# RWKV-7 recurrence on one core: each head's state placed by the head's parity instead of the chunk's, even and odd heads multiplied in turn, and values centred before the recurrence

## The chip, the core and the metric

The kernel runs on one NeuronCore of one Trainium2 chip. Its engines are TensorE (PE), VectorE (DVE), ScalarE (ACT), GpSimd (POOL) and SyncE (SP), which only issues transfers. The metric is device time in microseconds; lower is better. Instructions of one engine are executed in the order in which the program's scheduler has put them, so an instruction that waits holds up all that stand behind it on that engine.

## The reference

Two layers, each a token mixer and a dense SwiGLU, for 256 frames of width 2048 in fp32. The change lies in the first mixer, RWKV-7 with 32 heads of 64. A head keeps a 64x64 state S; every frame does

```
S_t = S_{t-1} diag(w_t) + (S_{t-1} a_t) b_t^T + v_t k_t^T      y_t = S_t r_t
mu  = mean(y);  var = mean((y - mu)^2)                          # over a head's 64 values
y   = (y - mu) * rsqrt(var + 64e-5) * lnx_g + lnx_b
y   = y + sum(r * k * r_k) * v                                  # the bonus, with the plain v
out = (y * g) @ w_o
```

S is linear in v, and so is y. If every v of a head has its mean over the head's 64 values taken off beforehand, y comes out with mean zero.

## The kernel before, in words

All weight products are GEMMs in split precision (`Stream.gemm`, lines 158 to 187): each block of 128x512 weights is cast to a rounded half (ACT, L149), the remainder is taken (DVE, L150), and three matmuls of 512 columns (L182 to L184) are made for each of two groups of 128 frames. Side work is written as generators that take a step after every three GEMM matmuls (`tick`), and the scheduler then fixes one order of instructions for each engine. Weights come in by transfers that SP issues (L194), half a megabyte each.

The recurrence is done in chunks of 64 frames by matrix products. The work is cut into 8 units, unit i being a group of 8 heads (512 columns) and a half of the frames (128 frames, that is two chunks c = 0 and 1). Four generators work on it, one unit behind the other:

- `prepare` (L565 to L673) makes the decays, the scaled keys and receptances, transposes them on PE (L635, L649), copies the transposes out of PSUM on ACT (L643 in eight copies, L654 in four) and multiplies them into one 128x128 block per head and chunk (L665, masked by DVE at L668 into `M`).
- `solve` and `merge` (L679 to L781) invert a triangular matrix per head and chunk with 32x32 products (L742, L749, L759, L775).
- `chain` (L792 to L848) carries the state. For each chunk: the block of M times the stacked tile `sv` (values on one half of the partitions, state on the other; L820), plus state times receptance (L823), a copy (ACT, L826), the inverse (L829), a copy (L831), the new state (L834, then DVE L841 or L843 and L844) and the output (L836, copied by L845).
- `post` (L850 to L901) norms each head's output (L858 to L888), transposes it (L896, L900), and `halve` splits it for the output GEMMs.

In `chain` the partition half depends on the chunk: `vs, us = half[c], half[1 - c]`. In chunk 0 all eight heads have their values on partitions 0 to 63 and their state on 64 to 127, in chunk 1 the other way round. So all eight products of L823, and all eight of L829, use the same half of the rows of the PE array and write the same half of the partitions:

```
for h, hs in enumerate(hsl):
    mm(pb[vs, hs], far[us, h, 0:C], sv[us, hs], start=h == 0, stop=False)      # L823
...
for h, hs in enumerate(hsl):
    mm(pu[us, hs], TT[us, h, :], vu[us, hs], start=True, stop=True)            # L829
```

`values` (L783) has SP load the values of a chunk twice (`sv`, `vu`), 64 rows of 512 each, from the DRAM copy `vdram`, which the GEMMs of v wrote (L529).

## Time and profile before

| | |
|---|---|
| runs | 2623.15, 2627.87, 2628.25 us; median 2627.87 us |
| profiled execution | 2622.87 us |
| its span, first to last instruction | 2621.1 us |
| PE busy | 2574.1 us (98%) |
| DVE busy, ACT busy | 1675.0 us (64%), 1481.8 us (57%) |
| the recurrence beside the first GEMMs of its output | from about 250 to 620 us of the span |

The profiled execution is shorter than the median by 5.0 us. Busy time of PE overlaps within itself: matmuls are pipelined, so the mean length of one matmul is longer than the distance from one to the next. How long a group of matmuls takes is therefore best read from the chain of work that ended last, which follows PE from start to start. An fp32 product is recorded as two matmuls, so eight products are x16.

### The profile page before, as it was taken

The numbers are of one execution on the slowest core, as the hardware profiler recorded it, in microseconds if no ns is written. First come the engines' busy times: TensorE is split into PE (matmuls) and PEld (weight loads), VectorE is DVE, ScalarE is ACT, GpSimd is POOL, SyncE is SP. The second block draws the span as 40 slices with busy tenths as digits, with TensorE's granted clock in tenths as the row PEclk, the third lists the DMA queues.
The fourth block names the chain that finished last, engine by engine and source line by source line (L and its number), as shares of the span: only waits on it lengthen the run. The fifth ranks groups of instructions, "written<-read, shape, count | busy, mean of one in ns | idle before, by whom it ended". The sixth has DMA issues, their size and how long they took to land.

```text
span 2621.1 us, 40943 instructions
## 1 busy us (share of the span) xinstructions
PE 2574.1 (98%) x15160; PEld 2110.4 (81%) x15160; DVE 1675.0 (64%) x2965; ACT 1481.8 (57%) x2869; POOL 92.2 (4%) x69
## 2 busy tenths in 40 slices
PE   7999999999999999999999999999999999999998
PEld 5788777778888888888888888888888888888887
DVE  7885888877555555555556677676755555555554
ACT  6665787876545454544455656555554545454444
POOL 0000010100000000000001010010000000000000
PEclk9999999999999999999999999999999999999999
DMA  6676323335666666655556666664666666665554
GB/s 193 181 212 215 111 86 102 105 114 154 192 186 192 187 192 186 192 193 192 189 190 205 201 201 185 184 203 155 188 189 189 190 188 192 187 192 190 195 193 161
DMA packets 253945, 468.46 MB, mean 179 GB/s; under 512 B 22248, under 2 KB 32696, under 8 KB 253744
## 3 DMA queue, kind: packets, MB, share of 16 engines
q1 hardware_dynamic: 250448, 463.10, 58.2%
q10 hardware_dynamic: 3136, 2.74, 0.3%
q8 instruction: 119, 1.95, 0.3%
q14 instruction: 82, 0.67, 0.1%
q0 software_dynamic: 160, 0.00, 0.0%
HBM read 457.37 MB, written 4.23 MB: 176 GB/s over the span
## 4 chain that ended last, share of the span: by engine, by line
PE 92%; ACT 4%; DVE 2%; issue 1%; DMA 1%; POOL 0%; SPq 0%; POOLq 0%; ACTq 0%; DVEq 0%
PE mm L182 28%; PE mm L184 28%; PE mm L183 28%; PE bg L997 1%; ACT xb L643 1%; PE bg L829 1%; DVE wl L150 1%; PE bg L820 1%; PE bg L665 1%; PE bg L836 1%; ACT Bs L867 1%; PE bg L312 1%; PE bg L834 1%; PE bg L823 0%; DVE xmf L376 0%
## 5 line engine op out<-in xcount | busy, mean ns | idle before, releaser
L150 DVE TENSOR_TENSOR wl<-st,wh 128x512 fp32r<-128x512 f32 (+1 forms) x1648 | 1129.8, 690 | 813.1 <-ACT wh L149 806.1
L149 ACT CAST wh<-st 128x512 fp32r<-128x512 f32 (+1 forms) x1648 | 1015.8, 622 | 952.2 <-DVE wl L150 697.3
L182 PE MATMUL mm<-wh,xb 128*128 128x512 f32 x2048 | 804.6, 393 | 0.0
L184 PE MATMUL mm<-wh,xb 128*128 128x512 f32 x2048 | 800.9, 391 | 0.0
L183 PE MATMUL mm<-wl,xb 128*128 128x512 f32 x2048 | 800.5, 391 | 0.0
L182 PEld LDWEIGHTS mm<-wh,xb 128*128 128x128 f32 x2048 | 385.0, 188 | 79.5 <-issue 3.3
L184 PEld LDWEIGHTS mm<-wh,xb 128*128 128x128 f32 x2048 | 384.8, 188 | 78.8
L183 PEld LDWEIGHTS mm<-wl,xb 128*128 128x128 f32 x2048 | 385.0, 188 | 75.9
L183 PE MATMUL mm<-wl,xa 128*128 128x512 f32 x768 | 305.3, 398 | 3.0 <-DVE wl L150 1.5
L182 PE MATMUL mm<-wh,xa 128*128 128x512 f32 x768 | 306.7, 400 | 0.0
L184 PE MATMUL mm<-wh,xa 128*128 128x512 f32 x768 | 305.0, 397 | 0.0
L184 PE MATMUL mm<-wh,hb 128*128 128x512 f32 x448 | 174.5, 390 | 0.0
L183 PE MATMUL mm<-wl,hb 128*128 128x512 f32 x448 | 174.5, 390 | 0.0
L182 PE MATMUL mm<-wh,hb 128*128 128x512 f32 x448 | 174.5, 390 | 0.0
L183 PEld LDWEIGHTS mm<-wl,xa 128*128 128x128 f32 x768 | 145.2, 189 | 33.0 <-DVE wl L150 3.2
L184 PEld LDWEIGHTS mm<-wh,xa 128*128 128x128 f32 x768 | 145.0, 189 | 30.0 <-issue 0.2
L182 PEld LDWEIGHTS mm<-wh,xa 128*128 128x128 f32 x768 | 145.4, 189 | 28.8 <-issue 1.0
L182 PEld LDWEIGHTS mm<-wh,hb 128*128 128x128 f32 x448 | 84.1, 188 | 17.5
L183 PEld LDWEIGHTS mm<-wl,hb 128*128 128x128 f32 x448 | 84.1, 188 | 17.5
L184 PEld LDWEIGHTS mm<-wh,hb 128*128 128x128 f32 x448 | 84.1, 188 | 17.3
L1181 POOL TENSOR_TENSOR n<-n,pw 128x8 f32<-128x8 f32 x24 | 47.2, 1968 | 409.0 <-DVE n L1180 409.0
L1224 ACT ACTIVATE sc<-sc,nm 128x128 f32<-128x128 f32 x64 | 28.7, 449 | 26.6 <-DVE nm L1223 26.6
(293 smaller groups left out, 1941.7 us busy)
## 6 DMA issues: line engine op xcount, KB each, us to landing
st<-in_f_w_gu_dram SPq DMA_DIRECT2D x352, 512.0 KB
st<-in_f_w_d_dram SPq DMA_DIRECT2D x176, 512.0 KB
st<-in_b_w_in_dram SPq DMA_DIRECT2D x128, 512.0 KB
st<-in_a_w_rkv_dram SPq DMA_DIRECT2D x96, 512.0 KB
st<-in_a_w_o_dram SPq DMA_DIRECT2D x32, 512.0 KB
st<-in_b_w_o_dram SPq DMA_DIRECT2D x32, 512.0 KB
cb<-cdram SPq DMA_DIRECT2D x4, 1024.0 KB
x<-in_x_dram SPq DMA_DIRECT2D x12, 256.0 KB
```

Of the source, the lines that this page charges most:

```text
L149: nc.scalar.copy(hi[:rows, :n], st)
L150: nc.vector.tensor_tensor(lo[:rows, :n], st, hi[:rows, :n].bitcast(F32), op=ALU.subtract)
L182: nc.tensor.matmul(ps[t][:, :n], xh[:rows, c], wh, start=b == 0, stop=False)
L183: nc.tensor.matmul(ps[t][:, :n], xh[:rows, c], wl, start=False, stop=False)
L184: nc.tensor.matmul(ps[t][:, :n], xl[:rows, c], wh, start=False, stop=b == kts - 1)
L312: nc.tensor.transpose(tp[:, i * T + t * P : i * T + (t + 1) * P], src[:, t, c : c + P], ident)
L643: nc.scalar.copy(dst, tpv[half[q], :, c, :])
L665: mm(pm[c][:, h * P : (h + 1) * P], fkb[us, b * 4 + h, :], far[us, b * 4 + h, :], start=True, stop=True)
L820: mm(pb[us, hs], M[:, c * 8 + h, C : 2 * C], sv[:, hs], start=True, stop=True)
L829: mm(pu[us, hs], TT[us, h, :], vu[us, hs], start=True, stop=True)
L1181: nc.gpsimd.tensor_tensor(n8[:, :], n8[:, :], pw[:, :], op=ALU.pow)
L1224: nc.scalar.activation(sc[:, c], sc[:, c], AF.Exp, bias=nm[:, t : t + 1], accum_out=nm[:, 2 + t : 3 + t])
```

## The change

A unit's head h = 2p + q has its state on partition half q, in both chunks, and its values on the other half. With that:

- the transposes come out of PE with even heads on one half of the partitions and odd heads on the other, which is where they are wanted, so that they are copied in 2 and 2 instructions instead of 8 and 4 (L661, L669 of the changed kernel), and the chunk's decay in 1 instead of 4 (L607);
- the products of L840 and L846 (before: L823, L829) are written in turn, an even head, an odd head, and so on (`turns`); the other products of the chain run over the four even heads and then over the four odd ones;
- what was one instruction on 64 rows of 512 becomes two on 64 rows of 4x64 for even and odd heads (kb, the state's update, the copies of the output, the loads of values), one copy becomes 128 rows of 256 (L844), and one is divided between ACT (L848) and DVE (L849);
- the values are centred once after the GEMM of v (`centred`), kept in a second DRAM array `wdram`, and the recurrence uses these. The norm then needs no mean: one square over 128x512, one reduction and one multiplication by the scale take the place of eight squares with a bias and eight scalings with a bias on ACT. The plain values are loaded again for the bonus (`vn`).

The diff, cut to its core:

```
+            def centred(vt, at):
+                v8 = vt[:, :].rearrange("p (h n) -> p h n", n=N)
+                m8 = lw.tile([P, 8], F32, name="m8")
+                nc.vector.tensor_reduce(m8[:, :], v8, AX.X, ALU.add)
+                nc.vector.tensor_scalar(m8[:, :], m8[:, :], -1.0 / N, None, op0=ALU.mult)
+                yield
+                wt = pre.tile([P, 2, T], F32, name="f2")[:, :, :].rearrange("p i n -> p (i n)")
+                nc.vector.tensor_tensor(
+                    wt.rearrange("p (h n) -> p h n", n=N), v8, m8[:, :].unsqueeze(2).broadcast_to([P, 8, N]), op=ALU.add
+                )
+                nc.sync.dma_start(wdram[at], wt)
...
-                    for c in range(2):
-                        for q in range(2):
-                            nc.scalar.activation(wc[half[c], q:8:2], pc[half[q], c:8:2], AF.Exp)
+                    nc.scalar.activation(wc[:, :], pc[:, 0:8], AF.Exp)
...
-                        nc.vector.scalar_tensor_tensor(
-                            kb[half[1 - c], c, :], kk[half[c], :], 0.5, Wi[half[c], :], op0=ALU.mult, op1=ALU.mult
-                        )
+                        for q in range(2):
+                            nc.vector.scalar_tensor_tensor(
+                                par(kb[half[q], c, :], q), par(kk[half[c], :], q), 0.5, par(Wi[half[c], :], q), op0=ALU.mult, op1=ALU.mult
+                            )
...
-                        for c in range(2):
-                            for q in range(2):
-                                dst = far[half[1 - c]].rearrange("f (p j) n -> f p j n", j=2)[:, :, q, j * C : (j + 1) * C]
-                                nc.scalar.copy(dst, tpv[half[q], :, c, :])
+                        dst = far.rearrange("f (c p) n -> f p c n", c=2)[:, :, :, j * C : (j + 1) * C]
+                        nc.scalar.copy(dst, tp[:, :].rearrange("f (p c t) -> f p c t", p=4, c=2))
...
-                        for q in range(2):
-                            dst = fkb[half[1 - c]].rearrange("f (p j) n -> f p j n", j=2)[:, :, q, :]
-                            nc.scalar.copy(dst, tkv[half[q], :, :])
+                        nc.scalar.copy(fkb[:, 4 * c : 4 * c + 4, :], tk[:, :].rearrange("f (p t) -> f p t", p=4))
...
-                a, b = u2.tile([P, 512], F32, name="sv"), u4.tile([P, 512], F32, name="vu")
+                a, b = u2.tile([P, 512], F32, name="sv"), u2.tile([P, 512], F32, name="vu")
                 r0 = t * P + c * C
                 for d in (a, b):
-                    nc.sync.dma_start(d[half[c], :], vdram[r0 : r0 + C, g * 512 : g * 512 + 512])
+                    for q in range(2):
+                        nc.sync.dma_start(par(d[half[1 - q], :], q), par(wdram[r0 : r0 + C, g * 512 : g * 512 + 512], q))
...
+                        heads = [(q, p, 4 * c + p, hsl[2 * p + q], slice(p * N, p * N + N)) for q in range(2) for p in range(4)]
+                        turns = [heads[4 * (j % 2) + j // 2] for j in range(8)]
-                        for h, hs in enumerate(hsl):
-                            mm(pb[us, hs], M[:, c * 8 + h, C : 2 * C], sv[:, hs], start=True, stop=True)
+                        for q, p, s_, hs, ps_ in heads:
+                            mm(pu[half[q], ps_], M[:, q * 8 + s_, C : 2 * C], sv[:, hs], start=True, stop=True)
                         if not first:
-                            for h, hs in enumerate(hsl):
-                                mm(pb[vs, hs], far[us, h, 0:C], sv[us, hs], start=h == 0, stop=False)
+                            for q, p, s_, hs, ps_ in turns:
+                                mm(pb[half[1 - q], ps_], far[half[q], s_, 0:C], sv[half[q], hs], start=p == 0, stop=False)
-                        nc.scalar.copy(vu[us, :], pb[us, :])
-                        for h, hs in enumerate(hsl):
-                            mm(pu[us, hs], TT[us, h, :], vu[us, hs], start=True, stop=True)
+                        u = u1.tile([P, 256], F32, name="u")
+                        nc.scalar.copy(u[:, :], pu[:, 0:256])
+                        for q, p, s_, hs, ps_ in turns:
+                            mm(pu[half[q], 256 + p * N : 256 + p * N + N], TT[half[q], s_, :], u[half[q], ps_], start=True, stop=True)
                         yield
-                        nc.scalar.copy(vu[us, :], pu[us, :])
+                        nc.scalar.copy(par(vu[half[0], :], 0), packed(pu[half[0], 256:512]))
+                        nc.vector.tensor_copy(par(vu[half[1], :], 1), packed(pu[half[1], 256:512]))
...
-                            mm(pb[vs, hs], M[:, c * 8 + h, 0:C], vu[:, hs], start=first, stop=first or h == 7)
+                            mm(pb[half[1 - q], ps_], M[:, q * 8 + s_, 0:C], vu[:, hs], start=first, stop=first or p == 3)
...
-                                nc.vector.tensor_tensor(new, pu[vs, :], sv[us, :], op=ALU.add)
-                                nc.vector.tensor_tensor(h4(new), h4(new), w, op=ALU.mult)
-                        nc.scalar.copy(Y[vs, :], pb[vs, :])
+                        for q in range(2):
...
+                                    nc.vector.tensor_tensor(new, old, par(sv[half[q], :], q), op=ALU.add)
+                                nc.vector.tensor_tensor(new, old, w, op=ALU.mult)
+                        for q in range(2):
+                            nc.scalar.copy(par(Y[half[c], :], q), packed(pb[half[1 - q], 0:256]))
...
+                vn = u1.tile([P, 512], F32, name="vn")
+                nc.sync.dma_start(vn[:, :], vdram[t * P : (t + 1) * P, g * 512 : (g + 1) * 512])
-                for h, hs in enumerate(hsl):
-                    nc.scalar.activation(y2[:, hs], Y[:, hs], AF.Square, bias=m8[:, h : h + 1], accum_out=r8[:, h : h + 1])
+                nc.scalar.activation(y2[:, :], Y[:, :], AF.Square)
+                nc.vector.tensor_reduce(r8[:, :], h4(y2[:, :]), AX.X, ALU.add)
-                for h, hs in enumerate(hsl):
-                    nc.scalar.activation(Y[:, hs], Y[:, hs], AF.Identity, scale=r8[:, h : h + 1], bias=m8[:, h : h + 1])
+                nc.vector.tensor_tensor(h4(Y[:, :]), h4(Y[:, :]), b8(r8[:, :]), op=ALU.mult)
```

The scheduler's order shows at three places what this moves. The first is PE in one chunk of the chain that is not a unit group's first. Before (L820, L823, L829, L834 and L836 as above; rows of GEMM matmuls between them):

```order
L820 MATMUL bg<-sv,xb_2535 64x64 x8
L823 MATMUL bg<-sv,xb_2535 64x64 x8
L184 MATMUL mm<-wh,xa_1478 128x512
L182 MATMUL mm<-wh,xa_1477 128x512
L183 MATMUL mm<-wl,xa_1477 128x512
L184 MATMUL mm<-wh,xa_1478 128x512
L829 MATMUL bg<-vu,TT_2551 64x64 x8
```

And in the changed kernel (L836 answers to L820 before, L840 to L823, L846 to L829, L852 to L834, L854 to L836):

```order
L836 MATMUL bg<-sv,xb_2580 64x64 x8
L840 MATMUL bg<-sv,xb_2580 64x64 x8
L846 MATMUL bg<-u,TT_2599 64x64 x8
L182 MATMUL mm<-wh,xa_1478 128x512
L183 MATMUL mm<-wl,xa_1478 128x512
L184 MATMUL mm<-wh,xa_1479 128x512
L854 MATMUL bg<-vu,xb_2580 64x64 x4
L182 MATMUL mm<-wh,xa_1478 128x512
L183 MATMUL mm<-wl,xa_1478 128x512
L852 MATMUL bg<-vu,xb_2580 64x64 x8
L854 MATMUL bg<-vu,xb_2580 64x64 x4
```

The inverse (L846) stands right behind the state product (L840) here, with no GEMM matmul between, since it now waits for L836 alone, and four output products of the even heads stand ahead of the state products L852.

The second is ACT from the norm of one unit to the preparation of the next. Before (L867 the squares, L643 and L654 the copies of the transposes, L882 the scaling):

```order
L867 ACTIVATE Bs,r_3893<-Y,m_3748 128x64 x7
L743 COPY Xs<-bg 128x256
L867 ACTIVATE Bs,r_3893<-Y,m_3748 128x64
L643 COPY xb_2534<-bg 64x4x64 x8
L654 COPY WW<-bg 64x4x128 x4
L149 CAST wh<-st 128x512
```

And in the changed kernel (L661 and L669 the copies of the transposes):

```order
L149 CAST wh<-st 128x512
L757 COPY Xs<-bg 128x256
L661 COPY xb_2580<-bg 128x4x2x64 x2
L669 COPY WW<-bg 128x512
L149 CAST wh<-st 128x512
L669 COPY WW<-bg 128x512
```

Twelve copies on half of the partitions have become four on all of them, and the eight squares are gone from ahead of them.

The third is DVE around the copy that the change gives to it (L849), in the changed kernel, with what each row waits for:

```order
L634 SCALAR_TENSOR_TENSOR WW<-kk,WW 128x512 [waits Activation_49]
L719 TENSOR_TENSOR E<-E 128x2x2 [waits DVE_49]
L150 TENSOR_TENSOR wl<-st,wh 128x512 [waits DMAHW6_49,Activation_49]
L723 TENSOR_REDUCE E<-E 128x2 [waits DVE_49]
L849 COPY vu<-bg 64x4x64 [waits Activation_49]
L719 TENSOR_TENSOR E<-E 128x3x3 [waits DVE_49]
```

The copy waits for ACT (for L848, the other half of the same copy), and stands in DVE's queue behind a remainder of weights (L150); before there was no instruction of DVE between L829 and L834.

## Rows read from the trace of the kernel before

**Rows 1.** The page: busy time of each engine over the span, and the engines' shares of the chain of work that ended last.

```profile
PE 2574.1 (98%) x15160; PEld 2110.4 (81%) x15160; DVE 1675.0 (64%) x2965; ACT 1481.8 (57%) x2869; POOL 92.2 (4%) x69
...
PE 92%; ACT 4%; DVE 2%; issue 1%; DMA 1%; POOL 0%; SPq 0%; POOLq 0%; ACTq 0%; DVEq 0%
```

**Rows 2.** Busy time in stretches of the span. Columns: start and end, length, then busy us (instructions) of PE, of its weight loads, of DVE, ACT and POOL, then PE's granted clock as a share of full speed, the share of the transfer engines, GB/s. The first row is the end of the GEMMs of v, the others the recurrence.

```profile
160.00:250.00 90.00, 89.77 (x417) 74.48 (x416) 53.28 (x90) 47.22 (x86) 3.17 (x5) 1.00 0.79 234
250.00:300.00 50.00, 47.54 (x296) 37.99 (x294) 42.42 (x83) 35.58 (x74) 2.31 (x2) 1.00 0.51 151
300.00:350.00 50.00, 47.43 (x863) 36.94 (x858) 40.55 (x86) 36.08 (x92) 4.90 (x4) 0.97 0.27 83
350.00:400.00 50.00, 47.13 (x661) 36.57 (x660) 40.66 (x94) 41.47 (x105) 6.31 (x5) 0.97 0.28 89
400.00:450.00 50.00, 49.14 (x718) 39.45 (x716) 39.45 (x85) 37.89 (x94) 5.59 (x5) 1.00 0.35 101
450.00:500.00 50.00, 47.81 (x923) 37.95 (x921) 42.79 (x97) 43.56 (x123) 5.20 (x4) 1.00 0.33 104
500.00:550.00 50.00, 48.57 (x691) 38.09 (x691) 42.27 (x89) 40.75 (x103) 6.16 (x5) 1.00 0.34 104
550.00:600.00 50.00, 48.26 (x696) 38.25 (x695) 30.61 (x69) 31.61 (x76) 1.94 (x1) 1.00 0.36 110
600.00:650.00 50.00, 48.99 (x233) 39.79 (x232) 42.50 (x79) 37.33 (x94) 3.24 (x2) 1.00 0.57 170
```

**Rows 3.** The chain of work that ended last, through one chunk: start us, us, what.

```profile
325.86 1.07 PE bg L820 x16
326.93 1.07 PE bg L823 x16
328.00 0.43 PE mm L183
328.43 0.24 PE mm L184
...
329.13 1.07 PE bg L829 x16
```

**Rows 4.** Groups of PE instructions by line: output<-inputs, rows*columns of the array, output shape, count | busy us, mean ns of one | idle us of PE just before them, and who ended it.

```profile
L823 PE MATMUL bg<-sv,xb 64*64 64x64 f32 x192 | 13.7, 222 | 0.0
L829 PE MATMUL bg<-vu,TT 64*64 64x64 f32 x256 | 18.3, 222 | 0.4 <-ACT vu L826 0.4
```

**Rows 5.** The same chain as in rows 3, other products on PE. L573: 128 columns of weights, 2 columns streamed. L635: transposes of 128x128. L742: 32x32, four heads' quarters of the array in turn. L759: 32x32, two quarters in turn. L665: 64 rows by 128 columns, the two halves of the rows in turn.

```profile
271.25 0.88 PE bg L635 x8
...
303.52 1.05 PE bg L742 x64
...
312.96 0.62 PE bg L759 x32
313.58 1.10 PE bg L665 x16
...
388.64 1.05 PE bg L573 x8
```

**Rows 6.** Groups by line as in rows 4: ACT's copies, squares and scalings of the recurrence, and the PE groups that waited for them.

```profile
L665 PE MATMUL bg<-xb,WW 64*128 64x128 f32 x256 | 28.4, 291 | 2.8 <-ACT WW L654 2.3
...
L643 ACT COPY xb<-bg 64x256 f32<-64x256 f32 x64 | 23.4, 366 | 3.1 <-PE bg L635 2.3
...
L882 ACT ACTIVATE Y<-Y,m,r 128x64 f32<-128x64 f32 x64 | 22.4, 428 | 1.7 <-DVE m L880 1.6
...
L654 ACT COPY WW<-bg 64x512 f32<-64x512 f32 x32 | 18.5, 580 | 0.8
...
L649 PE MATMUL bg<-cst,xb 128*128 128x128 f32 x64 | 10.1, 280 | 3.2 <-ACT xb L643 2.7 <-DVE xb L638 0.5
...
L831 ACT COPY vu<-bg 64x512 f32<-64x512 f32 x16 | 9.3, 581 | 13.6 <-PE bg L829 13.5
...
L743 ACT COPY Xs<-bg 128x256 f32<-128x256 f32 x16 | 5.9, 367 | 6.6 <-PE bg L742 6.5
...
L896 PE MATMUL bg<-cst,Y 128*128 128x128 f32 x32 | 5.5, 285 | 1.0 <-DVE Y L888 1.0
...
L577 ACT ACTIVATE rr<-kk 128x512 f32<-128x512 f32 x8 | 5.0, 628 | 1.8 <-DVE kk L575 1.8
...
L900 ACT COPY x<-bg 128x512 f32<-128x512 f32 x8 | 4.7, 584 | 0.6 <-PE bg L896 0.5
```

**Rows 7.** Groups by line as in rows 4: DVE on 64 rows of 512, on 128 rows of 256, and a reduction.

```profile
L628 DVE SCALAR_TENSOR_TENSOR xb<-kk,Wi 64x512 f32<-64x512 f32 x16 | 11.0, 686 | 0.5
...
L734 DVE TENSOR_TENSOR El<-Dg,cst 128x256 f32<-128x256 f32 x16 | 6.7, 420 | 1.5 <-PE bg L742 1.4
...
L858 DVE TENSOR_REDUCE m<-Y 128x8 f32<-128x512 f32 x8 | 5.4, 680 | 6.9 <-ACT Y L845 6.8
```

**Rows 8.** The same chain as in rows 3, at the end of the recurrence: the eight squares of the last unit.

```profile
599.83 1.05 ACT Bs L867 x6
...
601.08 1.52 ACT Bs L867 x9
```

**Rows 9.** Transfers. From the page: ACT's queue, the one with the smallest pieces (packets, MB, share of 16 engines' span). From the issues of line 789: duration ns min/median/max of issuing one, first and last start.

```profile
q10 hardware_dynamic: 3136, 2.74, 0.3%
...
L789 SPq DMA_DIRECT2D vu<-vdram x16: 445/451/588, 167.6 to 541.3; - x16
```

More of the change, by code (lines that the diff above doesn't have):

```diff
@@ L339, in hybrid_kernel @@
         vdram = dram.tile([T, D], F32, name="vdram")
+        wdram = dram.tile([T, D], F32, name="wdram")
         loraw = {}
@@ L528, in hybrid_kernel @@
                     nc.scalar.copy(vt[:, :], ps[t][:, :])
-                    nc.sync.dma_start(vdram[t * P : (t + 1) * P, g * 512 : (g + 1) * 512], vt[:, :])
+                    at = slice(t * P, (t + 1) * P), slice(g * 512, (g + 1) * 512)
+                    nc.sync.dma_start(vdram[at], vt[:, :])
+                    S.add(centred(vt, at))
             S.until(lambda: not S.act and not S.pend)
@@ L673, in prepare @@
                     done.add(("prep", i))
-            where = [(2, 0), (3, 0), (0, 1), (1, 1)]
+            where = [(0, 0), (1, 0), (2, 1), (3, 1)]
             quad = [slice(32 * q, 32 * q + 32) for q in range(4)]
@@ L796, in chain @@
                     if t == 0:
-                        nc.gpsimd.memset(nxt[0][half[1], :], 0.0)
+                        for q in range(2):
+                            nc.gpsimd.memset(par(nxt[0][half[q], :], q), 0.0)
                     yield from wait(("inv", i))
@@ L804, in chain @@
                     Y = u2.tile([P, 512], F32, name="Y")
-                    vus = []
                     for c in range(2):
@@ L817, in chain @@
                             nxt = values(*order[i + 1], 0)
+                        pu = yield from S.take()
                         pb = yield from S.take()
-                        for h, hs in enumerate(hsl):
-                            mm(pb[us, hs], M[:, c * 8 + h, C : 2 * C], sv[:, hs], start=True, stop=True)
+                        heads = [(q, p, 4 * c + p, hsl[2 * p + q], slice(p * N, p * N + N)) for q in range(2) for p in range(4)]
+                        turns = [heads[4 * (j % 2) + j // 2] for j in range(8)]
@@ L830, in chain @@
                         yield
-                        nc.scalar.copy(vu[us, :], pu[us, :])
-                        for h, hs in enumerate(hsl):
+                        nc.scalar.copy(par(vu[half[0], :], 0), packed(pu[half[0], 256:512]))
+                        nc.vector.tensor_copy(par(vu[half[1], :], 1), packed(pu[half[1], 256:512]))
+                        for q, p, s_, hs, ps_ in heads:
                             if not last:
-                                mm(pu[vs, hs], kb[:, c, hs], vu[:, hs], start=True, stop=True)
@@ L835, in chain @@
-                        for h, hs in enumerate(hsl):
-                            mm(pb[vs, hs], M[:, c * 8 + h, 0:C], vu[:, hs], start=first, stop=first or h == 7)
-                        if not last:
-                            new = nxt[0][vs, :]
-                            w = wc[vs, :].unsqueeze(2).broadcast_to([C, 8, N])
-                            if first:
-                                nc.vector.tensor_tensor(h4(new), h4(pu[vs, :]), w, op=ALU.mult)
-                            else:
-                                nc.vector.tensor_tensor(new, pu[vs, :], sv[us, :], op=ALU.add)
-                                nc.vector.tensor_tensor(h4(new), h4(new), w, op=ALU.mult)
@@ L845, in chain @@
-                        nc.scalar.copy(Y[vs, :], pb[vs, :])
+                                mm(pu[half[q], ps_], kb[:, c, hs], vu[:, hs], start=True, stop=True)
+                        for q, p, s_, hs, ps_ in heads:
+                            mm(pb[half[1 - q], ps_], M[:, q * 8 + s_, 0:C], vu[:, hs], start=first, stop=first or p == 3)
+                        for q in range(2):
+                            if not last:
+                                new, old = par(nxt[0][half[q], :], q), packed(pu[half[q], 0:256])
+                                w = wc[half[q], c:8:2].unsqueeze(2).broadcast_to([C, 4, N])
+                                if not first:
+                                    nc.vector.tensor_tensor(new, old, par(sv[half[q], :], q), op=ALU.add)
+                                    old = new
+                                nc.vector.tensor_tensor(new, old, w, op=ALU.mult)
@@ L846, in chain @@
+                        for q in range(2):
+                            nc.scalar.copy(par(Y[half[c], :], q), packed(pb[half[1 - q], 0:256]))
                         S.give(2)
@@ L862, in post @@
                 yield
-                yield
-                y2 = u1.tile([P, 512], F32, name="Bs")
                 r8 = u1.tile([P, 8], F32, name="r8")
-                for h, hs in enumerate(hsl):
-                    nc.scalar.activation(y2[:, hs], Y[:, hs], AF.Square, bias=m8[:, h : h + 1], accum_out=r8[:, h : h + 1])
-                yield
+                nc.vector.tensor_reduce(r8[:, :], h4(y2[:, :]), AX.X, ALU.add)
                 nc.vector.tensor_scalar(r8[:, :], r8[:, :], 1.0 / N, 64e-5, op0=ALU.mult, op1=ALU.add)
                 nc.gpsimd.tensor_tensor(r8[:, :], r8[:, :], pw[:, :], op=ALU.pow)
+                for _ in range(6):
+                    yield
                 yield
@@ L873, in post @@
                 yield
[L874 to L878 removed]
+                nc.vector.tensor_tensor(h4(y2[:, :]), h4(vn[:, :]), b8(bon[:, :]), op=ALU.mult)
                 nc.vector.tensor_tensor(y2[:, :], y2[:, :], vb[:, :], op=ALU.add)
[L880 to L882 removed]
+                yield
+                nc.vector.tensor_tensor(h4(Y[:, :]), h4(Y[:, :]), b8(r8[:, :]), op=ALU.mult)
                 nc.vector.tensor_tensor(Y[:, :], Y[:, :], vg[:, :], op=ALU.mult)
```

47 lines of the change are left out of this document (17 added, 30 removed).

## The prediction

> **What bounds the kernel now.** I read the page first: PE is busy for 98% of the span, and 92% of the chain that ended last is PE [rows 1]. DVE and ACT are far from full on the average. So time is won only where PE gets less to do or waits less, and the change touches PE between 250 and 620 us alone.
>
> Next the busy time by stretches, since an average says nothing of a stage [rows 2]. From 250 to 650 us PE is idle for 15.1 us (400 less the eight busy times), the largest pool of waiting in the program. DVE is busy for 278.8 us of the 350 from 250 to 600, 80%, and ACT for 266.9, 76%. In the stage just ahead (160 to 250) PE is idle for 0.2 us, and DVE has 36.7 us free.
>
> Third, the chain through one chunk, for the price of small products [rows 3]. Eight products of 64x64 (x16) take 1.07 us, that is 67 ns for each record. A GEMM matmul of 512 columns takes 0.23 to 0.24, but 0.43 when it is the first after a small group. So every return to the GEMM costs about 0.2 us.
>
> **PE's part: products in turn.** L823 has 192 records and L829 has 256 [rows 4]; the change writes both with even and odd heads in turn, so that neighbours use different halves of the rows and of the columns of the array. The other products keep all 128 rows and their number. Does turning pay? The trace has such products. L665 has the two halves of the rows in turn: 1.10/16 = 69 ns for each record of 128 columns. Whole-array products of the same width take 110 ns (L635) to 131 ns (L573) [rows 5]. So turning brings a factor between 0.625 and 0.524, and 67 ns would become 42 to 35. I take the middle, 38.5, since I can't tell which of the two is L665's true counterpart. The 32x32 products agree in kind: with two quarters of the array in turn 19.4 ns for each record, with four 16.4, so more parts do bring more. The gain is 448 x 28.5 ns = **12.8 us**, between 448 x 25 = 11.2 and 448 x 32 = 14.3. All of it lies on PE, so it counts fully.
>
> All these products in turn write one PSUM tile at a time (L742, L759) and are not slowed by it visibly. The Trainium skill, TensorEngine Tiling (Array Packing), Gotcha 1: PSUM Pressure, says that different row tiles cannot access the same PSUM bank at once. The even and the odd products go to one tile here, only to other partitions of it; by that rule as it stands the 12.8 us would be nothing, and the result would be that of the second case below. The trace's 16.4 ns for 32x32 products, whose four row tiles write one PSUM tile, speaks against applying it here.
>
> **PE's part: waits.** PE idled 2.3 us for L654 ahead of L665, 2.7 us for L643 ahead of L649, and 1.0 us ahead of the last L896 [rows 6]. For one unit the copies take 8 x 0.366 + 4 x 0.58 = 5.2 us on ACT; afterwards 4 x 0.584 (the row of 128x512) = 2.3 us. The wait ahead of L896 comes at the end of a norm whose eight squares alone take 2.8 us (599.83 to 602.60) [rows 8] and whose eight scalings take 22.4/8 = 2.8 us; one square of 0.63 us and one DVE instruction replace them. I take all three waits as gone: **6.0 us**. At the least nothing goes (the scheduler puts other work there), at the most all 15.1 us. The rest of the idle time I leave in place, because most of it has no releaser in the rows that the change shortens.
>
> Two costs on PE. The order of the changed kernel has 103 runs of GEMM matmuls in this stage instead of 95, since the output products are split in two: 8 x 0.2 = **1.6 us**. And the inverse (L846) now often stands right behind L840 without GEMM matmuls between. Its copy takes 0.37 us (128x256) [rows 6] with L840 as its cover; L840 in turn takes 16 x 38.5 = 0.62 us for non-first chunks, so in theory it suffices, with the hop between engines barely. I set **0.6 us** for the five or so places where it shows, bounds 0 and 5 x 0.37 = 1.9.
>
> **What stays off the path.** *ACT* gets lighter: copies of transposes 41.9 to 18.7 us, squares 22.4 to 5.0, scalings 22.4 to 0, the three copies of the chain 27.9 to 5.9 + 5.9 + 11.7 (half-size ones at 0.367), decays by 4: about 71 us less of 266.9. It is not the bound, so this is worth what PE waited for it, which is counted above.
>
> *DVE* gets heavier. An instruction on 64x512 takes 0.686 us and on 128x256 0.42 [rows 7]; the second is my value for 64x4x64. kb: 32 instructions become 64, 5 us more. State updates: 20 become 40, 3.1 more. New copies L849: 16 x 0.42 = 6.7. The bonus: 16 x 0.68 become 8 x 0.685, 5.4 less; the scaling by the norm 5.5 more. The reduction of squares takes the place of that of the mean (0.68), and small ones of 0.17 go, 2.8 in all. Sum +12 us in 350: from 80% to 87% of a slightly shorter stage. Its cover is PE's own GEMM work, with remainders made some blocks ahead; without that cover the 12 us would appear whole. Centring costs 8 x (0.68 + 0.17 + 0.69) = 12.3 us on DVE between 160 and 250, where 36.7 are free [rows 2]: nothing.
>
> *Transfers and SP.* Loads of values go from 32 to 64, at 0.45 us for each issue [rows 9]: 14.4 us more on SP in 350, plus 16 transfers for centred and plain values. Each load has 64 x 4 pieces of 256 bytes, 16384 pieces in all. The queue with the smallest pieces took 0.003 x 2621 x 16 / 3136 = 40 ns for each; that gives 41 us of all 16 engines, 12% on top of shares of 0.27 to 0.51 [rows 2]. Nothing, if loads still come a chunk ahead.
>
> **The sum.** -12.8 - 6.0 + 1.6 + 0.6 = -16.6 us. Against the profiled execution that is 2622.9 - 16.6 = 2606.3; the median of the runs stands 5.0 higher, so the forecast is 2627.9 - 16.6 = **2611.3 us**. Its own bounds: -11.2 + 0 + 1.6 + 1.9 and 2 us for DVE's load = -5.7, 2622; and -14.3 - 15.1 + 1.6 = -27.8, 2600, and some 4 us lower if the runs fall where the profiled execution of before did, 2596.
>
> **The rivals.** *The products in turn don't overlap* (0.11). Each product is two records, on the same part of the array, so the alternation is by pairs, and both write one PSUM tile. L665 has the same pairs and gains, which speaks against it, but it writes two PSUM tiles. Then -6.0 + 1.6 = -4.4: 2623.5 us, no change that counts.
>
> *The divided copy becomes the wait* (0.09, slower). Before, one ACT copy of 0.58 us [rows 6] stood between the inverse and the state product, covered by about four GEMM matmuls. Now an ACT copy of 0.37, then DVE's copy, which waits for it and stands behind a remainder of 0.69 on a DVE that is 87% full: 1.48 us with 0.42 for itself. PE has in the listed place 3 GEMM matmuls, 8 records of output products (0.54) and 2 more matmuls, 1.69 us, so it is just covered. If DVE is two or three instructions late, PE waits in each of 16 chunks, and the GEMM behind it too. From a mean wait of 1.4 us on (16 x 1.4 = 22.4, 5.8 more than the gain) the kernel is slower; with 1.8 us, 28.8 - 16.6 = +12.2, 2640 us. For it speaks DVE's load, against it that the scheduler put that much work between.
>
> *Values come late* (0.06). SP is in order, and the loads of `vu`, now with two buffers instead of four, wait for the products that read the old one, with loads of weights behind them. 15 loads each 1 us late cost 15 of the 16.6: 2626 us, no change.
>
> **How the numbers follow.** The forecast (2596 to 2622) has 0.74. To hold 8 in 10, the range takes in the case without overlap: 2596 to 2624. What is left out is 0.15. What a measurement of this kernel can tell from no change is about 0.2%, 5.3 us, so faster means under 2622.6: 0.74, and 0.03 from the edge of the second case, 0.77. Same: 0.08 + 0.06 = 0.14. Slower: 0.09.
>
> **What would show it.** In the profile of the changed kernel L840 x16 and L846 x16 should take about 0.6 us in the chain instead of 1.07, L836, L852 and L854 still 67 ns for each record; the four copies 2.3 us for one unit, with idle ahead of L667 and L679 near nothing; DVE about 87% from 250 to 590, and the end of the recurrence some 16 us earlier. The forecast is wrong in its main term if L840 and L846 still take 1.07, and in its cover if PE shows idle time ahead of L852 or L854 with L849 as releaser, or ahead of L836 with a transfer as releaser.

## The result and the profile after

| | before | changed |
|---|---|---|
| median (range) of 4 runs each | 2625.75 (2623.15 to 2628.25) us | 2604.48 (2597.18 to 2609.61) us |
| ratio, 95% interval | | 0.9914 (0.9895 to 0.9932) |
| profiled execution; its span | 2622.87; 2621.1 us | 2608.68; 2606.8 us |

Faster by 0.86% (0.68 to 1.05%), about 22 us. The profiled execution of the changed kernel lies at the slow end of its runs, so it shows only 14 us of that. The page, busy times and the engines' shares of the chain of work that ended last, as in [rows 1]:

```profile
PE 2558.9 (98%) x15160; PEld 2091.2 (80%) x15160; DVE 1693.5 (65%) x3041; ACT 1412.3 (54%) x2613; POOL 90.3 (3%) x73
...
PE 86%; DVE 6%; DMA 3%; ACT 2%; issue 1%; POOL 1%; ACTq 0%; SPq 0%; POOLq 0%; DVEq 0%
```

The stretches that answer to [rows 2] (same columns):

```profile
250.00:300.00 50.00, 46.56 (x295) 36.81 (x293) 45.10 (x96) 31.95 (x61) 2.31 (x2) 0.99 0.55 171
300.00:350.00 50.00, 48.94 (x937) 37.93 (x937) 45.44 (x101) 32.31 (x71) 6.46 (x4) 0.98 0.33 98
350.00:400.00 50.00, 47.77 (x780) 36.03 (x778) 42.55 (x106) 30.46 (x65) 4.73 (x6) 0.97 0.35 97
400.00:450.00 50.00, 45.84 (x855) 35.54 (x854) 42.85 (x98) 27.50 (x60) 7.07 (x6) 0.93 0.38 111
450.00:500.00 50.00, 49.04 (x745) 37.71 (x743) 45.53 (x102) 34.70 (x78) 4.50 (x5) 1.00 0.44 126
500.00:550.00 50.00, 48.81 (x743) 38.00 (x742) 46.41 (x113) 29.07 (x63) 3.51 (x3) 1.00 0.41 115
550.00:600.00 50.00, 48.02 (x563) 37.44 (x562) 37.47 (x69) 25.95 (x53) 3.89 (x2) 0.97 0.45 139
600.00:650.00 50.00, 50.00 (x237) 40.93 (x236) 35.24 (x61) 33.58 (x68) 0.70 (x1) 1.00 0.61 180
```

PE was idle for 15.1 us between 250 and 650 before, and it is idle for 15.0 us now (400 less the eight busy times). What changed is how much work PE gets through in that time. DVE went from 278.8 to 305.3 us of the 350 up to 600, that is 87%, and ACT from 266.9 to 211.9.

The chain of waits through a chunk, the answer to [rows 3]. It follows PE from start to start:

```profile
321.30 0.90 PE bg L836 x16
322.19 0.61 PE bg L840 x16
322.81 0.59 PE bg L846 x16
323.39 0.43 PE mm L182
...
324.29 0.61 PE bg L854 x8
324.89 0.43 PE mm L182
325.32 0.23 PE mm L183
325.56 0.72 PE bg L852 x13
...
326.45 0.29 PE bg L854 x5
```

Three things are to be seen. L840 and L846 take 0.61 and 0.59 us where L823 and L829 took 1.07. L836, whose products keep all 128 rows of the array and are not in turn, takes 0.90 instead of 1.07. And four output products of even heads (L854 x8) stand alone between GEMM matmuls and take 0.61 us, more than half of a whole group.

I then summed PE's timeline from start to start, from the first decay product to the first spread of the next mixer's input (L312), idle time apart. In the columns "idle" is PE's waiting by releaser; "issue" means that the profile names none.

| stage, us | before | changed | e1_again |
|---|---|---|---|
| length | 365.2 | 347.6 | 343.8 |
| L823, L829 (now L840, L846) | 30.1 | 17.0 | 17.0 |
| L820, L834, L836 (now L836, L852, L854) | 45.6 | 42.8 | 42.1 |
| L665 (now L679) | 26.9 | 22.1 | 22.3 |
| GEMM matmuls | 179.1 | 182.0 | 180.0 |
| idle: ACT, DVE, issue | 6.7, 2.8, 4.8 | 0.8, 5.6, 7.8 | 0.6, 4.7, 8.1 |

Outside the stage the profiled execution of the changed kernel is 3.3 us longer than that before, and that of e1_again (the changed kernel timed and profiled once more) 1.1 us shorter. So the gain is the products, 13.1 us, plus L665 and the products over all 128 rows (L836, L852, L854), 7 to 8 us, less 1 to 3 us more for the GEMM matmuls. It is not PE's recorded idle time: the waits for ACT went as forecast, and as much came in on DVE and without a releaser. Among the longest waits now are these, beside [rows 6] (engine, tile, line, releaser: us in total, times, longest):

```profile
PE bg L756 <- issue: 7.2, 3, 3.3
PE bg L773 <- DVE Ti L765: 2.1, 2, 1.1
PE bg L667 <- DVE xb L657: 1.2, 4, 0.6
PE bg L846 <- ACT u L844: 0.8, 2, 0.5
```

The 3.3 us among them are a wait too: PE stands until DVE has ended the first unit's inverse blocks (L730), as the timelines of the two engines show.

```profile
297.26 0.63 DVE L730 STREAM_TRANSPOSE Ti<-Xb 128x256 f32<-128x256 f32 x1
297.99 0.74 PE L756 MATMUL bg<-Ti,El 32*32 32x32 f32 x64 [3.27 <-issue]
```

### The profile page after: what moved, and what is told of

Read it like the earlier page. It is cut to its first block, busy times and chain, and to the rows that moved or that the text cites. A ratio compares the mean times of both kernels' runs of the same rounds, so it can differ in the third digit from the quotient of the medians.

```text
span 2606.8 us, 40879 instructions
## 1 busy us (share of the span) xinstructions
PE 2558.9 (98%) x15160; PEld 2091.2 (80%) x15160; DVE 1693.5 (65%) x3041; ACT 1412.3 (54%) x2613; POOL 90.3 (3%) x73
## 4 chain that ended last, share of the span: by engine, by line
PE 86%; DVE 6%; DMA 3%; ACT 2%; issue 1%; POOL 1%; ACTq 0%; SPq 0%; POOLq 0%; DVEq 0%
PE mm L182 26%; PE mm L183 26%; PE mm L184 26%; DVE wl L150 2%; DMA st<-in_a_w_rkv_dram 1%; DMA st<-in_b_w_in_dram 1%; ACT wh L149 1%; PE bg L1010 1%; PE bg L854 1%; PE bg L312 1%; PE bg L836 0%; DVE xmf L377 0%; PE bg L1246 0%; PE bg L846 0%; DMA st<-in_a_w_o_dram 0%
## 5 line engine op out<-in xcount | busy, mean ns | idle before, releaser
L150 DVE TENSOR_TENSOR wl<-st,wh 128x512 fp32r<-128x512 f32 (+1 forms) x1648 | 1127.9, 689 | 802.3 <-ACT wh L149 797.0
L182 PEld LDWEIGHTS mm<-wh,hb 128*128 128x128 f32 x448 | 84.1, 188 | 17.6
```

What stands on the lines that cost most here:

```text
L150: nc.vector.tensor_tensor(lo[:rows, :n], st, hi[:rows, :n].bitcast(F32), op=ALU.subtract)
L182: nc.tensor.matmul(ps[t][:, :n], xh[:rows, c], wh, start=b == 0, stop=False)
```

## The experiments

Each kernel is timed against the kernel before in five rounds, one chip for each series. The median of the kernel before was 2625.4, 2624.5, 2625.6 and 2625.4 us in the four series (e1, e2, e3, e5; e4, e6, e7, e8; e10, e14, e15; e16).

The times of one program's executions go mostly with the clock granted to TensorE. Of the 40 executions of the kernel before in these series the shortest, 2619.9 us, had a mean granted clock of 0.998, the longest, 2637.2 us, one of 0.990. An estimate from that: 0.001 of the clock is 2 to 3 us.

The last column counts the runs of GEMM matmuls in the scheduler's order, from the first decay product to the last transpose of the norm; the kernel before has 93.

| kernel | median (range), us | ratio to before (95%) | runs of GEMM matmuls |
|---|---|---|---|
| e1_again | 2604.9 (2600.5 to 2612.1) | 0.9926 (0.9909 to 0.9943) | 101 |
| e2_noturn | 2611.7 (2607.5 to 2615.4) | 0.9947 (0.9933 to 0.9961) | 101 |
| e3_allturn | 2600.5 (2597.4 to 2609.4) | 0.9906 (0.9890 to 0.9921) | 106 |
| e5_turnonly | 2606.3 (2604.6 to 2610.0) | 0.9928 (0.9915 to 0.9941) | 100 |
| e4_mean | 2606.4 (2602.4 to 2611.3) | 0.9927 (0.9911 to 0.9943) | 104 |
| e6_actcopy | 2595.4 (2589.9 to 2596.3) | 0.9878 (0.9863 to 0.9894) | 102 |
| e7_oddfirst | 2597.6 (2592.8 to 2601.5) | 0.9889 (0.9873 to 0.9905) | 92 |
| e8_pooladd | 2603.8 (2600.9 to 2609.3) | 0.9919 (0.9903 to 0.9934) | 110 |
| e10_oddeven | 2597.8 (2595.7 to 2604.2) | 0.9896 (0.9877 to 0.9915) | 86 |
| e15_allodd | 2591.2 (2589.7 to 2596.0) | 0.9870 (0.9848 to 0.9893) | 86 |
| e14_allodd_act | 2587.5 (2586.6 to 2594.4) | 0.9860 (0.9837 to 0.9883) | 93 |
| e16_lessdve | 2590.9 (2587.0 to 2591.6) | 0.9861 (0.9840 to 0.9882) | 96 |

**e1_again: the changed kernel once more.** Expected:

> The changed kernel once more, for its own spread and a second profile. Theory (the forecast's): products in turn -13 us, waits ahead of the transposes' products gone, two idle gaps of about 2 us each inside a run of 32x32 products come and go with the execution; so 15 to 25 us under the kernel before, L840 and L846 again about 38 ns a record. Rival (the gaps belong to this order of instructions): the same gaps at the same places, 2.1 us inside L756 near 437 us and 1.8 us near 554 us.

It fell where it had been, and both gaps inside L756 came again, 2.0 and 1.1 us long. Medians of one and the same program move by some us, those of the kernel before from 2624.5 to 2627.9, so differences under 3 us below decide nothing.

**e2_noturn: is it the turning?**

```
-  for q, p, s_, hs, ps_ in turns:      # L840 and L846
+  for q, p, s_, hs, ps_ in heads:      # four even heads, then four odd
```

> The changed kernel with L840 and L846 run over the even heads and then the odd ones, like the other products; nothing else. Theory (turning is the main term): L840 and L846 go back to 67 ns a record, 13 us slower than the changed kernel (11 to 15), about 2617. Rival (the gain is shorter ACT work and the turning is only visible in the rows): within 3 us of the changed kernel.

6.8 us slower than e1_again, half of what was expected. The timeline of e2_noturn shows why (start, length with the modelled end; distances from start to start):

```profile
347.06 0.96 PE L840 MATMUL bg<-sv,xb 64*64 64x64 f32 x16
347.95 0.50 PE L182 MATMUL mm<-wh,xa 128*128 128x512 f32 x1
```

The group takes 0.89 us, neither 1.07 nor 0.61. In all, L840 and L846 take 24.1 us there against 17.0 in e1_again: 7.1 us in the rows, 6.8 in the time. So in the rows, placing heads by parity with four even heads ahead of four odd ones brings 6 of the 13 us, and products in turn the other 7. One change of halves within the group saves 0.18 us, seven of them 0.46.

**e3_allturn: do products over all 128 rows gain from the turn?**

```
-  for q, p, s_, hs, ps_ in heads:      # L836, L852, L854
+  for q, p, s_, hs, ps_ in turns:
```

> All five groups of products of the chain in turn: L836, L852 and L854 too, which use all 128 rows and only half of the columns, other halves for even and odd heads. Theory A (only products on different rows overlap): those three stay at 67 ns a record, time within 3 us of the changed kernel, or up to 3 us more since the output products wait for both copies. Theory B (different column halves are enough): 704 records fall to about 40 ns, 19 us less than the changed kernel, about 2586.

They do: even and odd heads differ there only in the half of the columns, and the rows fell from 42.1 to 33.0 us. The time fell by 4.4 us only. The profiled execution lost time at the clock: it took 2609.4 us at a mean granted clock of 0.991, the other five 2597.4 to 2606.3 us at 0.993 to 0.996. Its stretches (columns as in [rows 2], PE's granted clock third from the end) and its timeline:

```profile
370.00:375.00 5.00, 3.73 (x78) 2.64 (x64) 3.47 (x9) 1.88 (x5) 2.26 (x2) 0.98 0.56 186
375.00:380.00 5.00, 4.93 (x25) 3.14 (x25) 4.43 (x9) 4.86 (x11) 1.14 (x1) 0.50 0.32 77
380.00:385.00 5.00, 5.00 (x53) 4.17 (x53) 3.11 (x7) 3.63 (x10) 0.00 (x0) 0.50 0.00 0
```

```profile
373.57 0.69 PE L773 MATMUL bg<-Ti,xb 32*32 32x32 f32 x32 [0.96 <-DVE Ti L765]
374.20 0.49 PE L679 MATMUL bg<-xb,WW 64*128 64x128 f32 x2
375.07 2.07 PE L679 MATMUL bg<-xb,WW 64*128 64x128 f32 x14 [0.39 <-DVE xb L682]
...
384.48 0.63 PE L184 MATMUL mm<-wh,gl 128*128 128x512 f32 x1
384.91 0.63 PE L182 MATMUL mm<-wh,gh 128*128 128x512 f32 x1
```

After two idle stretches PE runs at half its clock, the lower level of 1.2 GHz, and a GEMM matmul takes 0.43 us from start to start (384.48 to 384.91) instead of 0.23. Summed over the stage as (1 - clock) x 5 us, the profiles lost 3.4 us in the kernel before, 8.5 and 5.1 in the two of the changed kernel, 18.8 here. Since one program gives such different sums, this is one execution's price, not the kernel's, and where the rest of the 9 us went in the other executions is open.

**e5_turnonly: what are ACT's merged copies worth?** The placement and the turn stay; the transposes are copied as before (8 + 4 copies). The expectation says that plain values and the old norm were put back too. They were not: this kernel divides the copies alone, and ACT is busy for 234.3 us of 250 to 600 instead of 211.9.

```
-  nc.scalar.copy(dst, tp[:, :].rearrange("f (p c t) -> f p c t", p=4, c=2))
+  for c in range(2):
+      for q in range(2):
+          nc.scalar.copy(far[half[q], 4*c : 4*c+4, j*C : (j+1)*C], tpv[half[q], :, c, :])
```

> The changed kernel with the work that it takes off ACT put back: plain values, mean and bias in the norm (eight squares and eight scalings on ACT), and the copies of the transposes in eight and four pieces on half of the partitions. Placement and turning stay. Theory (forecast: ACT's relief is worth the 6 us that PE waited): 6 us slower than the changed kernel, with 2 to 3 us of idle each ahead of L665's and L649's counterparts. Rival 1 (idle only moved from ACT to DVE, as the total idle of the stage, 15.1 before and 15.0 after, says): within 2 us. Rival 2 (ACT's relief is worth more than PE's idle shows): 10 us or more.

1.4 us in the medians, less than can be told apart. Among PE's longest waits in e5_turnonly (L669 is L667, L682 is L679, L759 is L756 and L849 is L846 of the changed kernel):

```profile
PE bg L759 <- issue: 3.4, 2, 2.2
PE bg L849 <- ACT u L847: 1.8, 3, 0.8
PE bg L669 <- ACT xb L663: 1.5, 4, 0.4
PE bg L682 <- ACT WW L672: 1.1, 4, 0.3
```

ACT's waits are back at 6.5 us, DVE's are down to 2.2, the sum is 15.1 against 13.5 in e1_again. Waiting moved from one releaser to another. But the medians hide a difference in the clock. Five of the six executions had a granted clock of 0.998, the ten of the changed kernel 0.993 to 0.997; the means, 0.9977 and 0.9950, make some 7 us of 2605, by estimate. The two profiled executions, at 0.998 and 0.997, lie 6.0 us apart, 5.4 of it in the stage (349.2 against 343.8), and 3.0 of that is L682, that is L665. So in the rows the merged copies do save PE time, and by the estimate the lower clock takes most of it back; why the changed kernel is granted less is open.

**e4_mean: the norm with its mean, alone.** The eight squares and eight scalings return to ACT; the copies stay merged. e5_turnonly did not contain this part, as its expectation and this one suppose: the two kernels put back one part each, and none puts back both.

> The changed kernel with plain values in the recurrence, and so with the norm as it was (the mean's reduction on DVE, eight squares and eight scalings on ACT): ACT +40 us in the stage, DVE about -3 + 0. It parts centring from the merged copies, which e5_turnonly took back together at +1.4 us. If ACT's load matters for the last norm alone, as forecast: the wait ahead of the last transposes (1.0 us) comes back, +1 to +2 us on the changed kernel (2606). If ACT's relief is worth nothing: 2605, within 2 us. If it were DVE's 12 us for centring between 160 and 250 that cost something: 1 to 2 us faster (2603).

1.5 us slower than e1_again, within what can't be told apart, for some 36 us more on ACT (247.6 instead of 211.9 of 250 to 600). The wait for ACT did not come back: PE's idle time is 17.4 us, 10.2 with DVE and 1.3 with ACT as releaser.

**e8_pooladd: less work on DVE.**

```
-  nc.vector.tensor_tensor(y2[:, :], y2[:, :], vb[:, :], op=ALU.add)
+  nc.gpsimd.tensor_tensor(y2[:, :], y2[:, :], vb[:, :], op=ALU.add)      # and Y + y2
```

> The changed kernel with two of the six DVE instructions of 128x512 in the norm's tail (the bonus plus bias, and the sum of it with the scaled output) on GpSimd: DVE loses 16 x 0.69 = 11 us and falls to about 84% of 250 to 600. If DVE's load is what PE's new waits come from: these waits (L765, L682, L657 as releasers, 4 to 6 us in all) go to half, 2 to 4 us faster than the changed kernel (2601 to 2603). If they come from the length of the chain of a single unit and from gaps without a releaser: within 2 us. Rival: GpSimd takes over 1.5 us for each and stands in DVE's way or makes the norm end late: slower, 2608 or more.

1.1 us faster, nothing that counts; waits on DVE 6.4 us, not half of 5.6. It doesn't decide cleanly: the scheduler made 110 runs of GEMM matmuls of it, and DVE's scaling L895, 685 ns before, took 1110 ns beside GpSimd's 1.4 us additions.

**e6_actcopy: the second copy on ACT.**

```
-  nc.vector.tensor_copy(par(vu[half[1], :], 1), packed(pu[half[1], 256:512]))
+  nc.scalar.copy(par(vu[half[1], :], 1), packed(pu[half[1], 256:512]))
```

> The changed kernel with the second half copy of a chunk's u (L849) on ACT instead of DVE: DVE loses 16 x 0.42 = 6.7 us, ACT gains 16 x 0.37 = 5.9 us, and the two copies follow each other on one engine. If DVE's load is what refilled PE's waits: 2 to 4 us faster than the changed kernel (2601 to 2603). If the two engines side by side are needed (the divided copy stands on the path): 16 x 0.2 to 0.4 = 3 to 6 us slower (2608 to 2611), with PE idle ahead of L852 or L854. If neither, as the few waits there say: within 2 us.

9.5 us faster than e1_again, more than any theory had. PE's idle time is no shorter (13.6 us, 8.5 of it with DVE as releaser), but L852 and L854 take 22.7 us instead of 26.9. The scheduler now expects the copy earlier, and where L854 x8 stood alone it puts state and output products together: 3 such groups of eight records are left of 18. The profiled stage is only 3.7 us shorter than that of e1_again, so not all of the 9.5 us is placed.

**e7_oddfirst: the same products without the gap.** On e3_allturn:

```
+  odds = [heads[4 * (1 - j % 2) + j // 2] for j in range(8)]
-  for q, p, s_, hs, ps_ in turns:      # L852, L854
+  for q, p, s_, hs, ps_ in odds:
```

> The kernel of e3_allturn (all five sets of products of the recurrence in turn), but the state and the output products begin with the odd head, whose values the last of the two copies of a chunk brings. In e3_allturn the even product L854 was issued alone ahead of L852, so the GEMM was broken once more in most chunks. If these breaks and the gaps in them ate what turning the K=128 products gained: the same 0.5 to 0.6 us per 16 records, 8 to 15 fewer runs of GEMM matmuls at 0.2 us each, 2 to 3 us under e3_allturn (2598). If the loss of e3_allturn is in the clock after idle time and not in the breaks: within 2 us of it (2600).

2.9 us under e3_allturn, as the first theory had it, at the edge of what can be told; the products over 128 rows take 29.4 us instead of 33.0.

**e10_oddeven: order or engine?** The copy stays on DVE, nothing is put in turn:

```
-  for q, p, s_, hs, ps_ in heads:                        # L852, L854
+  for q, p, s_, hs, ps_ in heads[4:] + heads[:4]:
```

> The changed kernel, the second copy on DVE as it is, but the state and the output products take the four odd heads ahead of the four even ones (not in turn). Then no product can start before both copies, and the scheduler no longer puts four output products (L854) into a gap of their own ahead of L852: 86 runs of GEMM matmuls in the stage instead of 101. e6_actcopy was 9 us faster than the changed kernel, and its L852 and L854 took 22.7 us instead of 26.9. If that came from the order (the four products no longer alone): here too L852 and L854 below 24 us, and 5 to 9 us faster than the changed kernel (2596 to 2600). If it came from taking the copy off DVE: the time of the changed kernel within 2 us (2605), with idle time ahead of L852.

7.1 us faster than e1_again, with L852 and L854 at 24.3 us instead of 26.9 and the engine unchanged: the order. The profiled executions show less of it, 341.9 against 343.8 us of stage, at clocks of 0.995 and 0.997. In the timeline of e10_oddeven they stand together and nothing is alone ahead of them:

```profile
354.99 0.97 PE L852 MATMUL bg<-vu,xb 128*64 128x64 f32 x16
355.80 0.92 PE L854 MATMUL bg<-vu,xb 128*64 128x64 f32 x16
356.64 0.50 PE L184 MATMUL mm<-wh,xa 128*128 128x512 f32 x1
```

That is 0.81 + 0.84 = 1.65 us, where the changed kernel takes 0.61 for the four and 1.18 for the rest (325.56 to 326.74 in its chain), and one re-entry of the GEMM more.

**e15_allodd and e14_allodd_act: all in turn, odd head first,** with the copy on DVE and on ACT.

```
-  for q, p, s_, hs, ps_ in heads:      # L836, L852, L854; L840 likewise
+  for q, p, s_, hs, ps_ in odds:
```

> Copy on DVE, all four sets of products with a choice (L836, L840, L852, L854) in turn beginning with the odd head: 86 runs of GEMM matmuls, as e10_oddeven, but the K=128 products in turn. By the rows of e3_allturn these fall by 9 to 10 us (L836 15.9 to 12.9, L852 8.7 to 6.5, L854 18.2 to 13.7). If the rows reach the end of the stage once the breaks are away: 5 to 9 us under e10_oddeven, 2588 to 2592. If what PE saves is waited for elsewhere (DVE, gaps without a releaser, the clock after them): within 3 us of e10_oddeven.

> As e15_allodd, with the second copy on ACT: 93 runs of GEMM matmuls. If the gain of e6_actcopy came from the engine of the copy, this is 5 to 9 us under e15_allodd; if it came from the order alone, within 3 us of it or 1 to 2 us slower for the 7 more runs of GEMM matmuls at 0.2 us.

e15_allodd is 6.6 us under e10_oddeven, e14_allodd_act 3.7 us under e15_allodd. The first lies in the range expected, but the rows of the products over 128 rows fell by twice as much, from 39.4 to 26.7 us, while PE's idle time rose from 14.5 to 19.4. The second can't be told from no difference for certain, and it leaves open whether part of e6_actcopy's gain was the engine. A chunk in e14_allodd_act (L837, L841, L853, L855 answer to L836, L840, L852, L854):

```profile
354.77 0.68 PE L837 MATMUL bg<-sv,xb 128*64 128x64 f32 x16
355.38 0.68 PE L841 MATMUL bg<-sv,xb 64*64 64x64 f32 x16
355.99 0.50 PE L182 MATMUL mm<-wh,xa 128*128 128x512 f32 x1
...
359.31 0.69 PE L853 MATMUL bg<-vu,xb 128*64 128x64 f32 x16
359.83 0.64 PE L855 MATMUL bg<-vu,xb 128*64 128x64 f32 x16
360.39 0.50 PE L183 MATMUL mm<-wl,xa 128*128 128x512 f32 x1
```

The group of 16 takes 0.61 us over 128 rows as over 64, and state and output products 1.08 us together. With 2587.5 us this is the fastest version, 38 us (1.2 to 1.6%) under the kernel before.

**e16_lessdve: is it DVE's load?** On e14_allodd_act, four instructions of the norm's tail on 64 of the 512 columns; the other columns leave out bonus, scale and bias.

```
-  nc.vector.tensor_tensor(Y[:, :], Y[:, :], vg[:, :], op=ALU.mult)
+  nc.vector.tensor_tensor(Y[:, 0:64], Y[:, 0:64], vg[:, 0:64], op=ALU.mult)      # and three more
```

> e14_allodd_act, with scale, bias and bonus of the norm made on 64 of the 512 columns only (the other columns leave them out): 32 DVE instructions of 0.69 us shrink to some 0.15, 16 to 18 us less DVE work in the stage, without GpSimd beside it. 96 runs of GEMM matmuls instead of 93. In e14_allodd_act PE waits 10.6 us with DVE as releaser. If DVE's load is what these waits come from, as the waits of the changed kernel were explained after e1_again: they fall to about half, and the time by 4 to 6 us, to 2582. If they come from the length of one unit's own chain (what is relieved is waited for at the next instruction of the chain): 9 to 11 us again, and the time within 2 us of 2587.5.

No faster: 3.4 us slower in the medians, but 0.9861 of the kernel before against 0.9860 for e14_allodd_act. DVE is busy for 298 us of 250 to 600 instead of 307, and PE waits for it 12.0 us instead of 10.6:

```profile
PE bg L756 <- DVE Ti L765: 4.1, 5, 1.5
PE bg L756 <- issue: 3.3, 1, 3.3
PE bg L756 <- DVE Ti L730: 3.2, 4, 1.2
```

So 9 us less on DVE did not shorten the waits. Most stand at the 32x32 products, whose blocks DVE makes in many short dependent steps. That the length of this chain is the cause is what remains; it was not tried by itself.

## Why the prediction was right, and where not

The forecast was 2611.3 us, measured 2604.5, within its range and on its side. It was a gain of 16.6 us, counted from 2627.9, the median of three runs; from that of four, 2625.75, the gain measured is 21.3. The main term is right. Two others were too favourable, and two gains that were not in the forecast made up for them, so that the total came near is in part luck.

- **Products in turn, -12.8.** Right: 30.1 to 17.0 us, -13.1; 38 ns for each record. But not all is the turn: e2_noturn keeps 6 of it by the order of halves alone. The products share a PSUM tile and overlap all the same, so the second case of the prediction (no overlap) falls. By the rule of the Trainium skill, TensorEngine Tiling (Array Packing), Gotcha 1: PSUM Pressure, these groups would have stayed at 1.07 us; the trace, with 0.61, doesn't agree.
- **Waits, -6.0.** The step that failed. The three waits did go, each at its place: ahead of L667 and L679 nothing on ACT is left (of DVE 1.2 and 0.7 us), and nothing ahead of the last transposes; ACT's waits fell from 6.7 to 0.8 us in all. "The rest of the idle time I leave in place" was wrong: DVE's waits grew by 2.7 and those without a releaser by 3.0 us (1.5 of them at 298 us, where DVE is the one that is late), net -0.3 (e1_again -0.9). e5_turnonly puts back ACT's twelve copies for 1.4 us in the medians, e4_mean its squares and scalings for 1.5; both together were not tried. That the three engines hand PE work in turn, so that a wait taken from one is met again at the next, fits these rows; no run tests it by itself.
- **GEMM re-entries, +1.6.** Mis-sized. Eight more runs came, as forecast (101 for 93 by the count above). But L854 takes 17.6 us, more than the 16.5 of L836 in the kernel before, while L852 takes 9.3 for the 11.9 of L834. Splitting the output products to fill the wait for the second copy costs not only the re-entry but the end of a lone group of eight records, 0.61 us where its share of a whole group is half of 0.84. Without the split e10_oddeven is 7 us and e6_actcopy 9 us faster in the medians.
- **The copy of u, +0.6.** 0.8 us with L844 as releaser, against 0.4 for its counterpart before [rows 4].
- **Not forecast: products over all 128 rows.** "L836, L852 and L854 still 67 ns" failed: 0.90 us instead of 1.07 for sixteen, since the last even heads overlap the first odd ones; -2.8 us in all, after what the split cost L854.
- **Not forecast: L665.** It fell by 4.8 us with the same products. Before, the scheduler cut its 16 groups of eight into 25, often a single product in front of seven, because the copies came in halves; now there are 17. Cutting costs: a lone product took 0.41 us, a group of eight 1.09. But cuts are not all of it. With the copies divided again (e5_turnonly) the same products took 25.3 us in only 16 groups, 1.4 to 1.9 us for most. There the first records of a group follow each other at 112 ns until a copy on ACT (L672) releases the next; in the changed kernel two records pass in 112 ns from the start. So this gain is in part a wait for ACT as well, one that stands in the products' own time and not in the idle rows.
- **The rivals.** The divided copy as a wait did not come: no instruction of PE has L849 as releaser. Its cover was longer than worked out, 2.17 us in the chain (323.39 to 325.56) instead of 1.69: the sum took the two first GEMM matmuls at 0.23 and the lone group at 0.54, where the chain has 0.43 and 0.61. The copy cost through the order instead, which the split output products show. Values came in time: no wait of PE ahead of L836 with a transfer as releaser. DVE rose to 87% as worked out, at no price that e8_pooladd or e16_lessdve could show.

In the profiled execution the stage is 17.6 us shorter against 16.6 forecast; the medians are 21 us apart (20.6 for e1_again), the runs of the changed kernel spreading over 12 us.

## What to carry to other kernels

Before pricing the waits that a change removes, ask which engine hands PE its next work: in a stage where three engines alternate, PE's idle time never fell below 13 us in these kernels, and rose to 19 to 21 where its products were shortest. What was taken off PE's own products came through, but not always whole: 6.8 of 7.1 us by the turn (e2_noturn), 4.4 of 9.1 in e3_allturn, 6.6 of 12.7 from e10_oddeven to e15_allodd. Look at the granted clock of each execution too: two kernels whose medians agree can differ in the work and in the clock at once. Small products should stand together, in turn over halves of the array, and begin with the operand that comes last, so that the scheduler has no reason to send a few ahead. Count in the order how often each group is cut, not only how often the GEMM is entered.

## What the runs showed of the hardware

- Products that differ only in the half of the array's columns overlap as well as those that differ in rows and columns: sixteen records over 128 rows took 1.07 us all on one half of the columns, 0.81 to 0.90 with one change of halves, and 0.61 in turn (0.52 where another group over 128 rows follows).
- Apart from the one at 298 us, most gaps of 1.1 to 3.1 us in PE without a releaser lie in the middle of a run of like products, often at the same record from run to run (64 records of L756 cut after 59 in the changed kernel, e1_again, e2_noturn, e3_allturn, e7_oddfirst and e10_oddeven). In the changed kernel's timeline, and in its DMA queues from 437.0 to 437.5 us (packets, MB, share):

```profile
436.62 0.70 PE L756 MATMUL bg<-Ti,El 32*32 32x32 f32 x59
439.44 0.32 PE L756 MATMUL bg<-Ti,El 32*32 32x32 f32 x5 [2.12 <-issue]
```

```profile
q8 instruction: 1, 0.02, 11.8%
```

The queue for instructions moves a packet just as PE stops, and so it does ahead of the gaps at 556 us there and at 306 and 572 us in the kernel before. It moved 40 packets between 250 and 625 us in the changed kernel, so one just ahead of each of these four gaps is more than chance would give. The products of 32x32 pass at 12 ns for each record. That PE waited for its own code is a reading of these rows; no run tested it.
